# Attention with grouped heads on one core: a new instruction order, and the last head's norm and store in two halves

## The chip, the core and the metric

The kernel runs on one core of a Trainium2 chip. The core has a matrix engine (PE, TensorE), a vector engine (DVE, VectorE), an activation engine (ACT, ScalarE), a general engine (POOL, GpSimd) and a queue engine (SP, SyncE) that mostly issues DMAs. Each engine works through its own instructions in order and waits on semaphores for the others.

The metric is device time in microseconds (us), the median of several executions. Times inside an execution come from one profiled execution; its span runs from its first to its last instruction.

## What is computed

Softmax attention over 8 batches, 8 query heads and 2 key/value heads, a sequence of 1024 and a head size of 64, in float32 at the interface. Four query heads share one key/value head.

```python
scores = scale * np.matmul(q_group, k_group.transpose(0, 1, 3, 2))
scores_max = np.max(scores, axis=-1, keepdims=True)
attn = np.exp(scores - scores_max)
attn = attn / (np.sum(attn, axis=-1, keepdims=True) + 1e-08)
output[:, q_start:q_end, :, :] = np.matmul(attn, v_group)
```

The kernel leaves the maximum out, works in bfloat16 on the way, and gets the row sums from a column of ones beside V.

## The kernel before

**Heads and pairs.** There are 64 heads (batch times query head), numbered 0 to 63. A head's scores are made key-side first, in 8 pairs of 128 x 512 matmuls: one pair gives a 128 x 1024 tile `sp` in PSUM, and there are three such score buffers. So there are 512 score pairs. Each goes to one of two engines for its exponential:

- ACT: one exp activation (L764) into `pt`.
- DVE: a bit trick. One pass over the scores (L775, "dpass") writes 16-bit whole numbers `yt`. Two passes of up to 1024 scores form a *chain*, which is then finished in 16-bit steps: `zh` (L782, mantissa into `zt`), `two` (L789, exponent into `et`), `mul` (L798, `zt = yt * zt`) and, for the last `TAIL` heads alone, `add` (L803, `zt = et + zt`). The other heads have no add: PE multiplies both `et` and `zt` with V and so adds them in PSUM.

**Part of `mul` on GpSimd.** GpSimd can take columns of a chain's `mul` off DVE (L732, "gmul"). Its parts are placed beside a DVE pass, and beside a norm that follows it, and their widths are worked out by `gpsimd()` of the planner:

```python
until = t + window + M_GOVER
at += M_GLEAD
...
w = int((until - at - M_GFIX) / M_GCOL) // GSTEP * GSTEP
```

Here `window` is 1134 for a pass, plus `M_NORM` (531) where a norm follows, plus `M_REC` where it begins at a reciprocal. A part waits for the DVE instruction placed ahead of it.

**PV.** The probabilities are the stationary side of 128 x 65 matmuls with V (L816), for 8 pieces of 128 queries a head. Pieces are gathered by seven in one PSUM bank (`ops`), by four for the first head. A finished group gets a reciprocal of its sums (L881, "rec") and a multiplication (L890, "norm") into the ring `ost`, from which SP stores whole heads (L894). The first head (L836) and the last one (L856) are worked by key chunk rather than by piece. The last head's eight pieces lie in a freed score buffer, get one reciprocal and one norm of 128 x 512, and one store of 256 KB on SP's queue.

**The order.** A planner (`Plan`) replays the kernel with constants for the engines' costs (`M_ACT`, `M_REC`, `M_FIX`, ...), and reads from the text `ORDER` what PE and DVE do next. Letters of PE: `A` a score pair for ACT; `a` to `d` a score pair for DVE, of the current head or one to three heads on; `V` a group of PV matmuls; `E` and `L` the PV of the first and last head; `F` a filler matmul; `W` a planned wait. Letters of DVE: `p` and `P` a pass (`P` where a norm follows); `r` and `R` a reciprocal; `n` a norm; `0` to `3` the next step of that open chain; `i` idling. `x` closes an open chain. `W` and `i` issue nothing. What comes out is a list of events in planned time; the program is emitted in that order, so each engine's sequence is fixed, while the semaphores set the real times. DMA loads (GpSimd's cast copies `q`, `k`, `v`, SP's transposes and copies) and stores are placed by planned times as well.

Of the kernel before, what the change touches and what calls it, by code (L numbers as in the profile page):

```python
# [29 lines left out]
M_D1 = 1.042  # L30
M_D2 = 0.521
M_D4 = 0.261
M_REC = 90
M_GLEAD = 160
M_GFIX = 190
M_GCOL = 1.88
M_GOVER = 100
M_GLATE = 900
M_GFREE = 125
M_ISSUE = 850  # L40
M_OVER = 5000
NEED = 5150
M_GFREE = 125
M_OVER = 5000
NEED = 5150
M_NORM = 531
# [3 lines left out]
PB = 7  # L50
NPIECE = 8
GRAIN = 3
TAIL = 4
CHN = 2
LONG = 6
GFROM = 2
# [5 lines left out]


ORDER = """
AaApFFFFFWFFAWWWWWWWWWWWWWWWWWWWWaWWWWWWWWWWApEEWWAW0WWWbWWWWApEEWWAWW0WWWaEpAEWWA0WWAFWWWWbFF0FE0AE
pAWWWWWWWAR0AWWWWWWWWWaWWWnWWWWWWpWWWWAVVVVVVARnb0VVVVpAVVVVVA0aWWWWApVVVVVVVVAR0AVb0VVVPVVAVVVVnVVA
b0VVVpAVVVVVA0AWWW0WbVVVRVpVVVVAVVVnVVA0bWWWApVVVVVVVVA0AWW0WbVVVRVPVVVVAVVVnVVA0bWWWApVVVVVVVVA0cWW
0WAVVVRVPVVVVAVVVnVAb0WWWWWApVVVVVVVVA0AWW0WWcVVVRpVVVVVAVVnVVVA0bWWWApVVVVVVVVA1cWWWArVPVVVVVVVAnWc
WWA0VpVVVVVVVA0WWcWWApVVVVVVVVAR0AWWWc0VVVVVPVAVVVVVcnAVpVVVAVVV1WVVAcR0WWWWAVPVVVVVVVAnWWAWc0V1VVVV
VpVVAVVVA0bVRVPVVAVVVVVnAA0WVVVV1VVVVVV0AV0VVVVAbVRVPVAVVVVVVVnVAb0WWAVpVVVVVVVVVA0WWWbWA0VVVVVRVPVV  # L70
VAVVVVbnAVpVVVAVVVVV0VVAc1VVVApVVVVVVVA1WbWWWApVVVVVVVVVVA0r1bWWAPVVVVVVVVVAncW0WWAVVVV0VVARVPVVVVVV
AWWnWWWWbA1VVVVVpVVAVVVA1bVRVPVVVAVVVVnVAA00VVVVVAW0WbVVVpVVVVVVAVVrV0cAVpVVVVVAVV0VVAb0VVVVAPVVVVVV
VAncWWW0WAVVVVpVVVVAVVV0VAb0VVVRVpAVVVVVAnbWWW0WAVVVpVVVVAVVVRV1Ab1VVVVAPVVVVVVAnWbWWA0ipVVVVVVVVAR1
cVV1VAVPVVVVAVVVnVVA0bWWWApVVVVVVVVAR1cWWWAPVVVVVVVVVAnbWW0WAVVpVVVVVVVAVV0VVAAR1VVVVVnVVVVVV1cAVpVV
VVVVVA0WWWbWAVpVVVVVVVARWW1WbWWAVPVVVVVVVAnWWcWWA0VVV0VVVVVApVVVVVARW1WbWWAVPVVVVVVVAnWWcWWA0VVVpVVV
VVAVVRV1bAVPVVAVVVVnVAA0VVVV0VVVV0cWAVpVVVVVVVVARW1WbWWAVPVVVVVVVVVAnWcWWA0VVVVpVVVVVVAVV0VcARVPVVVA
VVVnVVA1bVVVpVAVVVVVA01cWWWApVVVVVVVVA0cVARPVVVVVVAnWAV0VVVVV1cWApVVVVVVVVA0cWWWA1VVVVRVPVVVAVVVVnVA
c0WWWApVVVVVVVVAR1cWWWAPVVVVVVVVAnAV1VVVVVVVc2AVpVVVVVVVVVArW0Wc1WWAVVVPVVVVVVAVVnVVVA2cVVpAVVVVVAR0
bVVPVAVVVVVVnAV2AAV1VVVV0VVVVVVA1bVRVPVVVVVAVVnVVVA0cVVVpAVVVVVAR1bWWWAPVVVVVVVVAncWWWA1VVVpVVVAVVVV
0VA1cVRVPVVAVVVVVVnVAa1WWWAVpVVVVVVVVVA0WWWcA1VVVVVpVVVVAVVVVV0VVAbWWWARpVVVVVVVAnAV1VVVVVV0VVVVA0cV  # L80
VVRVPAVVVVVVAnaWW0WWAVVVpVVVVVVAVV0VVA0bVVVVRPVVAVVVVAnWAV0VVVVVVV0bWAVpVVVVVVVARW0WbWAVPVVVVVVVAnWW
bWA0VVVVVpVVVVAVVVV0VVARb0WWWAVPVVVVVVVVVAnWWAWb0VVVVVpVVVAVVVVV0VVARb0WWWWAVPVVVVVVVAnWWbWWA0VVVVpV
VVAVVVV0VVA0bWWWARVPVVVVVVVAnWWbWWA0VVVVpVVVVAVVV0VVA0bWWWARVpVVVVVVVAnWbWWA0VVVVpVVAVVVVV0VVARb0WWW
AVPVVVVVVVAnWWaWWA0VVVVVpVVVVAVVVV0Aa0VVVVVpAVVVVVVAR0WbVVAPVVVVVVVAnAV1VVVVVV0VVAR0aVVVPVVAVVVAnbVi
VipVVVAVVVV0Ab0VVVVVApVVVVVVA0WbWWApVVVVVVVVVVAR1bWWWAPVVVVVVVVVAncWW0WAVpVVVVVVVA0WAVVRV1VVVVVVnVAb
1VVVVpAVVVVVA0bWWWARPVVVVVVVVAnbWWW1WAVVV1VVVVApVVVVVVA0WWbWWARpVVVVVVVVAnaWW1WAVVVpVVVVVAVV0VA0bVVV
RAPVVVVVVAnaV1AVVpVVVVAVVV0VVVAR0bWWWAPVVVVVVVVAnAV1VVVVVVV1VaAipVVVVVVVVVVA0WbWWARPVVVVVVVVVVAnAV1V
VVVVV1bWApVVVVVVVVVARW0WbWWWAPVVVVVVVVAnWbVV1VAVpVVVVVVAV0VVVVA0bWWRWAPVVVVVVVVAnAV1VVVVV1VVbAipVVVV
VVAWWRWW0WcAPVVVVVVVVAnWAWWWb1VVVVpVVVVAVVV0VVAR0cWWWAPVVVVVVVVAnWAWWWb1VVVV1VVVVApVVVVVAW0WWWcWARpV
VVVVVVVAnWcWWWA1VVVVpVVVVAVVV0VVA0cWWWARPVVVVVVVVAnbWWWA1VVVV1VVVVApVVVVVARWW0WbWAPVVVVVVVVAncWWWA1V  # L90
VVpVVVVVAVV0VVVAR0bWWWAPVVVVVVVVAnAV1VVVVVc1WAVpVVVVVVVA0WWbWARPVVVVVVVVAnWAV1VVVVVVb0WAVVpVVVVVVVVA
WW0WWWWcAVRPVVVVVVVAVnVVVb1AVVVpVVAVVVVA1cV0VVpAVVVVVVA1aWWWWARPVVVVVVVVAnbWWW1WAVVVpVVVVAVVVrV2AAnV
VVVV0VV1VVVVA0bVVVVVApVVVVVVVARWnWbWAVpVVVVVVVVVA0WAWWWA0VVVVVV0VVVVVVVrVnVbA0VVVVVVVVVApVVVVVAVV0VV
VAaVVVpVVAVVVVVV0AbWWWArPVVVVVVVVA0AVVnVVVVV0VVVVAAV0VVVVVVVVVVVARnaVVVpVAVVVVVVVVRA0AVnVVVVVV0VVVVV
VA0AVVVVVVVRVV0VVVVVVVVAanWWAVpVxVVVVVVVVVVAR0AWnWAVVV0VVVV0VVVVVL0LLLRnLLLLFFRFn
"""


# [339 lines left out]
def kernel(  # L438
# [7 lines left out]
    nc = tc.nc  # L446
# [239 lines left out]
    for x in [e for e in plan.ev if e[1] == "norm"]:  # L686
        lo, hi = x[2]
        for j in range(NJ - 1):
            if lo < (j + 1) * NPIECE <= hi:
                ev.append((x[0] + 700, "store", None, j, None))  # L690
        if lo >= plan.last:
            ev.append((x[0] + 1, "store", None, NJ - 1, None))
    order = {id(e): i for i, e in enumerate(ev)}
    ev.sort(key=lambda e: (e[0], order[id(e)]))

# [27 lines left out]
    for when, kind, x, j, c, *cols in ev:  # L723
# [101 lines left out]
        elif kind == "pvf":  # L825
            first = j == NC - 1
            if first:
                new_bank(0)
                new_bank(1)
            for i in range(NPIECE):  # L830
                par = i % 2
                ci = x if par == 0 else (x + NH) % NC
                every = [p for _, p in terms(0, par, [ci])]
                lo = i % 4 * (D + 1)
                for n, p in enumerate(every):
                    nc.tensor.matmul(  # L836
                        ops[i // 4][:, lo : lo + D + 1],
                        lhsT=p[:, i // 2 * 128 : (i // 2 + 1) * 128],
                        rhs=va[0][:, ci % NH, ci // NH, :],
                        start=(first and i % 4 == 0 and n == 0),  # L840
                        stop=(j == 0 and n == len(every) - 1),
                        skip_group_check=True,
                    )
        elif kind == "pvl":
            b, h = divmod(NJ - 1, H)
            first = j == NC - 1
            if first:
                new_slot(plan.spare)
            for i in range(NPIECE):
                par = i % 2  # L850
                every = [
                    (ci, p) for ci, p in terms(NJ - 1, par) if ci == (x if par == 0 else (x + NH) % NC)
                ]
                lo = i % 4 * (D + 1)
                for n, (ci, p) in enumerate(every):
                    nc.tensor.matmul(  # L856
                        sps[plan.spare][:, i // 4, lo : lo + D + 1],
                        lhsT=p[:, i // 2 * 128 : (i // 2 + 1) * 128],
                        rhs=va[(b * G + h // HPG) % NVA][:, ci % NH, ci // NH, :],
                        start=(first and i % 4 == 0 and n == 0),  # L860
                        stop=(j == 0 and n == len(every) - 1),
                        skip_group_check=True,
                    )
        elif kind in ("rec", "norm"):
            lo, hi = x
            n = hi - lo
            r = place_of(lo)
            if lo < plan.last:
                o = ops[plan.group_of[lo] % 2][:, 0 : n * (D + 1)]
                o = o.rearrange("p (s d) -> p s d", d=D + 1)  # L870
                sums = o[:, :, D]
            else:
                o2 = sps[plan.spare][:, :, 0 : 4 * (D + 1)]
                o2 = o2.rearrange("p b (s d) -> p b s d", d=D + 1)
                sums = o2[:, :, :, D]
            if kind == "rec":
                rec = rp.tile([128, NPIECE], FP32, name="rec")
                to = rec[:, 0:n]
                if lo >= plan.last:
                    to = to.rearrange("p (b s) -> p b s", b=2)  # L880
                vec = nc.vector.reciprocal(out=to, in_=sums)  # L881
            else:
                to, by = ost[:, r : r + n, :], rec[:, 0:n].unsqueeze(2).to_broadcast([128, n, D])
                if lo < plan.last:
                    o = o[:, :, 0:D]
                else:
                    o = o2[:, :, :, 0:D]
                    to = to.rearrange("p (b s) d -> p b s d", b=2)
                    by = by.rearrange("p (b s) d -> p b s d", b=2)
                vec = nc.vector.tensor_tensor(out=to, in0=o, in1=by, op=ALU.mult)  # L890
        elif kind == "store":
            b, h = divmod(j, H)
            r = place_of(j * NPIECE)
            ins = nc.sync.dma_start(  # L894
                out=rows(out[b, h], j in (0, NJ - 1)),
                in_=ost[:, r : r + NPIECE, :].rearrange("p (s two) d -> p s (two d)", two=2),
            )
            stores.append((when, ins))
# [30 lines left out]
```

## Time and profile before

| | us |
|---|---|
| median of 3 runs | 354.96 (354.9 to 355.17) |
| the profiled execution | 354.69 |
| its span | 352.9 |
| first exp on ACT starts | 6.22 |
| last matmul of the last head ends (L856) | 348.86 |
| last norm ends (L890) | 349.83 |

The time around the span (354.69 against 352.9) lies outside the instructions. The clock granted to PE was 1.000 over the whole execution. Share of the engines in the chain that ended last: DVE 67%, PE 21%, ACT 8%.

The forms of GpSimd's parts, which the sum of the change draws on (line, engine, operation, tiles, shapes and count | busy us, mean ns of one | idle before, releasers):

```profile
L732 POOL TENSOR_TENSOR zt<-yt,zt 128x464 bf16<-128x464 bf16 x66 | 70.1, 1063 | 53.7 <-DVE et L789 25.6 <-DVE zt L782 12.4 <-DVE zt L798 8.9
L732 POOL TENSOR_TENSOR zt<-yt,zt 128x800 bf16<-128x800 bf16 x28 | 47.5, 1698 | 25.4 <-DVE rec L881 14.9 <-DVE zt L782 3.9 <-DVE et L789 3.8
L732 POOL TENSOR_TENSOR zt<-yt,zt 128x752 bf16<-128x752 bf16 x28 | 45.0, 1608 | 24.9 <-DVE zt L782 15.9 <-PE sp L754 4.8 <-DVE et L789 3.4
```

How to read it: an engine's instruction may be issued before the record of the one ahead of it has ended, so records of one engine overlap a little, and the time an instruction costs is the distance from its start to the next start.

### The profile page before, as it was taken

What the parts mean: (1) busy time and instruction counts of PE and PEld (TensorE: products, weight loads), DVE (VectorE), ACT (ScalarE), POOL (GpSimd) and SP (SyncE); (2) the same over time, 40 slices, a digit from 0 to 9 for tenths busy, and PEclk for the clock granted to TensorE, in tenths of its full rate; (3) what the DMA queues carried; (4) which work ended last, traced back from release to release, by engine and by line L of the source; (5) the groups of instructions that cost most, each with busy time, mean ns of one, the idle gap of its engine ahead of it and who ended that gap; (6) DMA issues with size and microseconds to landing.
All of it is one profiled execution on the core that took longest, in us unless ns stands there. A gap on an engine that the chain in (4) does not pass through costs nothing.

```text
span 352.9 us, 14128 instructions
## 1 busy us (share of the span) xinstructions
PE 344.6 (98%) x6247; PEld 223.8 (63%) x6247; DVE 344.3 (98%) x519; ACT 344.3 (98%) x373; POOL 204.1 (58%) x188
## 2 busy tenths in 40 slices
PE   8899999999999999999999999999999999999995
PEld 4456666666666666666666666666666666666664
DVE  4999999999999999999999999999999999999995
ACT  5999999999999999999999999999999999999994
POOL 3157656676577666676766566666657676663000
PEclk9999999999999999999999999999999999999999
DMA  6799666478866987669639756679567885454133
GB/s 150 133 151 151 135 124 136 91 141 146 133 126 124 140 157 132 120 115 154 154 61 181 138 124 115 135 108 180 109 114 130 165 141 112 101 101 114 27 93 121
DMA packets 96430, 44.84 MB, mean 127 GB/s; under 512 B 61152, under 2 KB 95072, under 8 KB 95584
## 3 DMA queue, kind: packets, MB, share of 16 engines
q1 hardware_dynamic: 94128, 31.48, 43.1%
q0 software_dynamic: 2096, 12.19, 24.0%
q8 instruction: 49, 0.80, 1.1%
q10 hardware_dynamic: 144, 0.26, 0.2%
q14 instruction: 13, 0.11, 0.1%
HBM read 27.13 MB, written 28.97 MB: 159 GB/s over the span
## 4 chain that ended last, share of the span: by engine, by line
DVE 67%; PE 21%; ACT 8%; issue 3%; DVEq 0%
DVE yt L775 35%; PE ops L816 10%; DVE et L789 8%; PE sp L754 8%; ACT pt L764 8%; DVE zt L798 7%; DVE ost L890 7%; DVE zt L782 7%; DVE rec L881 2%; PE ops L619 1%; PE sp L856 1%; PE sp L642 0%; DVE kt L663 0%; PE ops L654 0%; PE ops L642 0%
## 5 line engine op out<-in xcount | busy, mean ns | idle before, releaser
L764 ACT ACTIVATE pt<-sp 128x1024 bf16<-128x1024 f32 x369 | 341.8, 1034 | 0.5 <-PE sp L754 0.4
L732 POOL TENSOR_TENSOR zt<-yt,zt 128x464 bf16<-128x464 bf16 (+5 forms) x131 | 173.4, 1324 | 107.7 <-DVE et L789 35.5
L816 PE MATMUL ops<-va,pt 128*128 128x65 bf16 x2848 | 175.1, 194 | 0.0
L754 PE MATMUL sp<-qt,kt 64*128 64x512 bf16 x1024 | 171.0, 382 | 3.2 <-ACT pt L764 1.5
L775 DVE TENSOR_SCALAR yt<-sp 128x1024 uint16<-128x1024 f32 x143 | 172.6, 1207 | 0.6 <-PE sp L754 0.5
L816 PEld LDWEIGHTS <-pt 128*128 128x128 bf16 x2848 | 127.7, 97 | 31.9 <-issue 31.9
L816 PE MATMUL ops<-va,zt 128*128 128x65 bf16 x1120 | 130.9, 194 | 0.0
L816 PE MATMUL ops<-va,et 128*128 128x65 bf16 x1072 | 121.7, 194 | 0.0
L816 PEld LDWEIGHTS <-zt 128*128 128x128 bf16 x1120 | 89.9, 97 | 12.3 <-issue 12.1
L816 PEld LDWEIGHTS <-et 128*128 128x128 bf16 x1072 | 84.2, 98 | 20.6 <-issue 20.6
L754 PEld LDWEIGHTS <-kt 64*128 64x128 bf16 x1024 | 49.2, 93 | 54.8 <-issue 32.5
L782 DVE TENSOR_SCALAR zt<-yt 128x2048 uint16<-128x2048 uint16 x72 | 50.1, 696 | 0.1
L789 DVE TENSOR_SCALAR et<-yt 128x2048 uint16<-128x2048 uint16 x72 | 49.6, 691 | 0.0
L798 DVE TENSOR_TENSOR zt<-yt,zt 128x832 bf16<-128x832 bf16 (+7 forms) x69 | 45.1, 654 | 0.0
L890 DVE TENSOR_TENSOR ost<-ops,rec 128x448 f32<-128x448 f32 (+2 forms) x73 | 44.3, 607 | 0.2
L517 POOL DMA_DIRECT2D qd<-in_q_dram x33 | 20.2, 613 | 4.2 <-PE sp L754 3.3
L881 DVE RECIPROCAL rec<-ops 128x7 f32<-128x7 f32 (+2 forms) x73 | 14.2, 195 | 0.0
L517 POOL DMA_DIRECT2D kd<-in_k_dram x8 | 5.4, 670 | 5.4 <-PE sp L754 5.4
L619 PE MATMUL ops<-warm 128*128 128x128 bf16 (+1 forms) x23 | 4.5, 339 | 1.2 <-DVE warm L511 1.2
L517 POOL DMA_DIRECT2D vd<-in_v_dram x8 | 5.0, 621 | 0.2 <-issue 0.2
L803 DVE TENSOR_TENSOR zt<-et,zt 128x2048 bf16<-128x2048 bf16 (+1 forms) x4 | 4.4, 1090 | 0.1
L619 PEld LDWEIGHTS <-warm 128*128 128x128 bf16 x23 | 2.0, 114 | 3.7 <-issue 2.5
(38 smaller groups left out, 25.2 us busy)
## 6 DMA issues: line engine op xcount, KB each, us to landing
out_dram<-ost SPq DMA_DIRECT2D x64, 256.0 KB, 3.1
qd<-in_q_dram POOLq DMA_DIRECT2D x29, 256.0 KB, 5.0
kt<-kt SPq DMA_DIRECT2D x30, 64.0 KB, 3.1
va<-vd SPq DMA_DIRECT2D x30, 64.0 KB, 3.7
kd<-in_k_dram POOLq DMA_DIRECT2D x7, 256.0 KB, 5.6
vd<-in_v_dram POOLq DMA_DIRECT2D x7, 256.0 KB, 5.2
qt<-qd SPq DMA_TRANSPOSE x63, 4.5
qd<-in_q_dram POOLq DMA_DIRECT2D x5, 128.0 KB, 3.7
```

What stands on the lines that cost most here:

```text
L517: return nc.gpsimd.dma_start(out=t.rearrange("(a x) d -> a (x d)", a=128), in_=src.rearrange("(a x) d -> a (x d)", a=128),)
L619: nc.tensor.matmul(ops[bank][:, lo : lo + cols], lhsT=warm[:, 0:128], rhs=warm[:, 0:cols], start=not beside, stop=True, skip_group_check=b ...
L732: gps = nc.gpsimd.tensor_tensor(out=z, in0=flat(yt[j])[:, lo : lo + w], in1=z, op=ALU.mult)
L754: now = nc.tensor.matmul(sps[x][:, half, :], lhsT=t[lo : lo + D, c // NH, ci % NH * 128 : (ci % NH + 1) * 128], rhs=qt[j][lo : lo + D, 0, ...
L764: exps.append(nc.scalar.activation(out=p, in_=where_s[(j, c)], func=AF.Exp, scale=scale))
L775: vec = nc.vector.tensor_scalar(out=yt[ch][:, i, :, :], in0=where_s[c], scalar1=EXP_A, scalar2=EXP_B, op0=ALU.mult, op1=ALU.add,)
L782: vec = nc.vector.tensor_scalar(out=zt[j][:, 0:c], in0=yt[j][:, 0:c], scalar1=0x7F, scalar2=0x3F00, op0=ALU.bitwise_and, op1=ALU.bitwise_or,)
L789: vec = ins = nc.vector.tensor_scalar(out=et[j][:, 0:c], in0=yt[j][:, 0:c], scalar1=0x7F80, scalar2=None, op0=ALU.bitwise_and,)
L798: vec = nc.vector.tensor_tensor(out=z, in0=flat(yt[j])[:, 0 : cols[0]], in1=z, op=ALU.mult)
L816: nc.tensor.matmul(ops[plan.group_of[x] % 2][:, lo : lo + D + 1], lhsT=p[:, qs * 128 : (qs + 1) * 128], rhs=va[(b * G + h // HPG) % NVA][: ...
L881: vec = nc.vector.reciprocal(out=to, in_=sums)
L890: vec = nc.vector.tensor_tensor(out=to, in0=o, in1=by, op=ALU.mult)
```

## The change

Three constants of the planner get other values: `M_REC` 90 to 115, `M_GOVER` 100 to 60, `M_GFREE` 125 to 85 (this one is the time by which a part may reach into the next DVE operation before the plan counts it as a delay). `TAIL` goes from 4 to 3, so head 60 loses its `add` step, and its `et` goes to PE. The text `ORDER` is a new one throughout. The last head's norm becomes two instructions of 128 x 256, one for each PSUM bank, and each is followed at once by its own store of 128 KB, the first on SP's queue, the second on ACT's; the store event of the last head is gone.

```diff
-M_REC = 90
+M_REC = 115
...
-M_GOVER = 100
+M_GOVER = 60
 M_GLATE = 900
-M_GFREE = 125
+M_GFREE = 85
...
-TAIL = 4
+TAIL = 3
...
 ORDER = """
-AaApFFFFFWFFAWWWWWWWWWWWWWWWWWWWWaWWWWWWWWWWApEEWWAW0WWWbWWWWApEEWWAWW0WWWaEpAEWWA0WWAFWWWWbFF0FE0AE
...
-VAaVVVpVVAVVVVVV0AbWWWArPVVVVVVVVA0AVVnVVVVV0VVVVAAV0VVVVVVVVVVVARnaVVVpVAVVVVVVVVRA0AVVnVVVVVV0VVVVV
-VA0AVVVVVVVRVV0VVVVVVVVAanWWAVpVxVVVVVVVVVVAR0AWnWAVVV0VVVV0VVVVVL0LLLRnLLLLFFRFn
+AaApFFFFWWWWFAWWWWWWWWWWWWWWWWWWWWWWWWWWWWaWWWWWWWWWWApEEWWAW0WWWbWWWWApEEWWAW0WWWaWWWWApEEWWA0WWbFF
...
+VVVVV0b0VVApVVVVVVVVAR0bWWWWAPVVVVVVVVVAnbW0WWAVVpVVVVVVAV0VVAARnVVVVV0VVVVVVVVA1AVVV1VVVVVV0VAAVVV
+RVV0VVVVVVVVAnAVVV0VVVVVVVVVVVVVVRAnaWWWApVVVVVVVVVxVA0ArVnVVVVVVV0VA0AVVV0VVVVVLLRnLLLLLWWLFFRFn
 """
...
-        if lo >= plan.last:
-            ev.append((x[0] + 1, "store", None, NJ - 1, None))
...
-                to, by = ost[:, r : r + n, :], rec[:, 0:n].unsqueeze(2).to_broadcast([128, n, D])
                 if lo < plan.last:
-                    o = o[:, :, 0:D]
+                    parts = [(nc.sync, 0, n, o[:, :, 0:D])]
                 else:
-                    o = o2[:, :, :, 0:D]
...
-                vec = nc.vector.tensor_tensor(out=to, in0=o, in1=by, op=ALU.mult)
+                    n //= 2
+                    parts = [(e, i * n, n, o2[:, i, :, 0:D]) for i, e in enumerate((nc.sync, nc.scalar))]
+                for e, i, m, src in parts:
+                    by = rec[:, i : i + m].unsqueeze(2).to_broadcast([128, m, D])
+                    to = ost[:, r + i : r + i + m, :]
+                    vec = nc.vector.tensor_tensor(out=to, in0=src, in1=by, op=ALU.mult)
+                    if lo >= plan.last:
+                        e.dma_start(
+                            out=rows(out[B - 1, H - 1], True)[:, i // 2 : (i + m) // 2, :],
+                            in_=to.rearrange("p (s two) d -> p s (two d)", two=2),
+                        )
```

Counts of letters in the two texts, which say how often each thing is done:

| | before | after |
|---|---|---|
| `A` (scores for ACT) | 369 | 370 |
| `a` to `d` (scores for DVE) | 143 | 142 |
| `0` to `3` (chain steps) | 220 | 219 |
| `p`, `P` (passes) | 89, 54 | 83, 59 |
| `r`, `R` (reciprocals) | 7, 67 | 4, 70 |
| `V` (PV groups) | 1616 | 1608 |
| `W` (planned waits of PE) | 406 | 436 |
| `F` (fillers) | 14 | 13 |

More of the change, by code (lines that the diff above doesn't have):

```diff
@@ L42 @@
 NEED = 5150
-M_GFREE = 125
+M_GFREE = 85
 M_OVER = 5000
@@ L64 @@
 ORDER = """
-AaApFFFFFWFFAWWWWWWWWWWWWWWWWWWWWaWWWWWWWWWWApEEWWAW0WWWbWWWWApEEWWAWW0WWWaEpAEWWA0WWAFWWWWbFF0FE0AE
[L66 to L94, printed above, removed]
@@ L95 @@
-VA0AVVVVVVVRVV0VVVVVVVVAanWWAVpVxVVVVVVVVVVAR0AWnWAVVV0VVVV0VVVVVL0LLLRnLLLLFFRFn
+AaApFFFFWWWWFAWWWWWWWWWWWWWWWWWWWWWWWWWWWWaWWWWWWWWWWApEEWWAW0WWWbWWWWApEEWWAW0WWWaWWWWApEEWWA0WWbFF
+WAFFpFEAWWW0WWWAAE0W0WWWWWWWWWWWWWWWaRAnWWWWRWWWPWAVVVVVVVVnA0bWWWWApVVVVVVVVA0aWVpAVVVVVAR0bVVA0VVV
+pVVVAVVVVnVAb0VVVApVVVAV0VVVVA0bVVRVPVAVVVVVAnbV0AVpVVVVVAVV0VVA0bVVRVPVAVVVVVAnbW0WWAVVpVVVVVVAV0VV
+VVA0bWWRWAPVVVVVVVVAnbW0WWAVVpVVVVAVVV0VVVVA0cWWWRWAPVVVVVVVVAnbW0WWAVVVpVVVAVVV0VVVVAR0cWWWAPVVVVVV
+VVAnbWW0WWAVVVpVVVVVAVV0VAc0VVVRVPAVVVVAnVA0WbVVVpVVVVAVVV0WVVA0bWWWWARPVVVVVVVVAncWWWA0VVVpVVVAVVVV
@@ new lines @@
+0VVA0bVVArPVVVVVVA0WcWWWAPVVVVVVVVAnAV0VVVV0VVVARb0VVVVPVVVAVVVVcnAVpVVVVVAVV0VVAb0VVVVRVAPVVVVVVAnW
+cWWWA0VVVVpVVVVAVVV1VVAc0VARVPVVVVVVAWnWWWbA0VVVVVpVAVVVVVV0VAc0WWWAVpVVVVVVVA0WbWWARVPVVVVVVVAnWWcW
+WA1VVVV0VVApVVVVVVVARWnWbWWApVVVVVVVVA0WcWWWApVVVVVVVVVA1cWWWARPVVVVVVVVVVAncWW1WAVVV2VVVVApVVVVVVVV
+VA00WcWWAVVRVPVVVVVAVVnVVVA1bWWWWApVVVVVVVVA0cWWRWAPVVVVVVVVAncWW01WWAVVpVVVVVVAWV0VcA1VVVVpVAVVVVAR
+0AVVc1VVVPVVVAVVVVnVAc1WWWWAVpVVVVVVVARWW0WcWWAPVVVVVVVVVAnWAV1VVVVVVVV1VcARVPVVVVVVAVnVVVA0cV1VVVVA
@@ new lines @@
+pVVVVVAW1WWWcWApVVVVVVVVA0cWWWARVPVVVVVVVAnWWcWWA1VVVVpVVVVAVVVVR0VAc1WWWAVPVVVVVVVAnWWcWA0VVVVVpVVV
+AVVVVRV0Ac1WWWAVPVVVVVVVAWnWWWcA0VVVVVpVVVAVVVV2AAV0VVVVVV0VbWWARPVVVVVVVVVVAncWWWA1VVVVpVVVVVAVVVVr
+V2VAc2WWWAVPVVVVVVVAnWWWbWA0VpVVVVVVVARWW2WcWWAVPVVVVVVVAnWWbWWA0VVVVpVVVVAVVV0VVAAWWRWWc0VVVVPVVVVA
+VVVnVAA1VVVVV1VVVVVA0bVVVVRVPVVVVAVVVVAnc1VVVApVVVVVVVVA1WWbWWApVVVVVVVVVVAR0c1WWWAVVPVVVVVVAVVnVVVV
+VA0bVVVpAVVVVVAR1bWWWWAPVVVVVVVVAncWW0WWAVVpVVVVVVAVV0VA1bVRVPVVAVVVVVnAA0VVVVV1VVVVVA0bVVpVAVVVVVVR
@@ new lines @@
+A1AVnVVVV1VbWWAipVVVVVVVVA0cWWWARPVVVVVVVVVAnbWWWA1VVVVpVVVVVAVVVV0cA0VVVVApVVVVVVVAR1AVVVnVVVVb1WWA
+VpVVVVVVVVA0WcWAVpVVVVVVVVAR0AWWWbVV0VVVVAPVVVVVVVAncWWARPVVVVVVVAnWWAV1VVVVVV0cWAVpVVVVVVVA1WAWWcRV
+nVVVVVpVVAVVVA01cVVpVAVVVVVV0AAWWW0WcVVVRVPVVVVAVVVnVVA1cWWWApVVVVVVVVA1AWWWbR0VVVVPVVVVAVVVnVVA1cWW
+WApVVVVVVVVAR0WcWWWAPVVVVVVVVAnAV1VVVVVb0WAVpVVVVVVVARW0WcWWAPVVVVVVVVAnbWWWA1VVV0VVVVVApVVVVVVA0WcW
+ARVPVVVVVVVVAnWAV1VVVVVVb0WWAVpVVVVVVVVVARW0WbWWAPVVVVVVVVVVAnAV1VVVVVVb0WAVpVVVVVVVVVARW0WAWWb0VVVV
@@ new lines @@
+VVPVVAVVVVVVVnVAb1WWAVpVVVVVVVA0WWbWARVPVVVVVVVAnWWAV1VVVVVV0VVVA1bVVVpVVAVVVVA0WbVRVPVVVAVVVVVAnA1W
+VVVVVV1VVcAipVVVVVVVVA0WWbVRAPVVVVVAnVVA1bVV1VVVVApVVVVVVA0WbWWARPVVVVVVVVAnAV1VVVVVb1WAVpVVVVVVVARW
+0WaWWAPVVVVVVVVAnbWWWW1WAVVVpVVVVVAVV0VVVA0aWWARPVVVVVVVVVAnAV1VVVVVVVb1AVpVVVVVVVVVARWW0WbWAPVVVVVV
+VAVnVVVVVV1VAb1WWWWAVpVVVVVVVVVA0WWbWARVPVVVVVVVVAnWWbWWA1VVVVVpVVVVAVVV1bAVpVVVVAVV0VAr1cVVPVVAVVVV
+AnAV1VVVVV0VVbARVpVVVVVVAWnWWWcWA1VVVVVpVVVAVVV0VVA0bWWWApVVVVVVVVAR1AWWWc1VVVVVPVVVAVVVVnVAb0WWWAVp
@@ new lines @@
+VVVVVVVARW1WAWWcV1VVVVVPVVAVVVVVnAc0WWWAVpVVVVVVVARWW1WbWAVPVVVVVVVAnWWcWA0VVVVpVVVAVVVV0cAVRpVVAVVV
+VVnVAb1WWWWApVVVVVVVVA0cWWWRWAPVVVVVVVVAnbWW1WWAVVVpVVVVVAVV0VVVARc0WWWAPVVVVVVVVAnbWW1WAVVVpVVVVVVA
+VV0VVAA0VVVV1VVVVVVVRc0AVPVVVVVVVAVnVVVA0bVVVApVVVVVVVVAR1AVVVnVVVVVV0VVVVA1aVVVpVAVVVVVVA0bWWWWARPV
+VVVVVVVAnbWWW1WAVVV1VVVApVVVVVVVA0WbWWARPVVVVVVVVAnbWWW1WAVVVpVVVVVAVV1VAA0VVV0VVVVVVVVVVARnbVVVVpVA
+VVVVVA0b0VVApVVVVVVVVAR0bWWWWAPVVVVVVVVVAnbW0WWAVVpVVVVVVAV0VVAARnVVVVV0VVVVVVVVA1AVVV1VVVVVV0VAAVVV
@@ L882 @@
             else:
-                to, by = ost[:, r : r + n, :], rec[:, 0:n].unsqueeze(2).to_broadcast([128, n, D])
                 if lo < plan.last:
-                    o = o[:, :, 0:D]
+                    parts = [(nc.sync, 0, n, o[:, :, 0:D])]
                 else:
-                    o = o2[:, :, :, 0:D]
-                    to = to.rearrange("p (b s) d -> p b s d", b=2)
-                    by = by.rearrange("p (b s) d -> p b s d", b=2)
-                vec = nc.vector.tensor_tensor(out=to, in0=o, in1=by, op=ALU.mult)
+                    n //= 2
[9 more added lines that the diff above has]
+                        )
         elif kind == "store":
@@ L894 @@
             ins = nc.sync.dma_start(
-                out=rows(out[b, h], j in (0, NJ - 1)),
+                out=rows(out[b, h], j == 0),
                 in_=ost[:, r : r + NPIECE, :].rearrange("p (s two) d -> p s (two d)", two=2),
```

## The prediction

> **What bounds the kernel now.** I read the page's busy shares first, then its groups, the waits, the timeline, and last the end of the span.
>
> ```profile
> PE 344.6 (98%) x6247; PEld 223.8 (63%) x6247; DVE 344.3 (98%) x519; ACT 344.3 (98%) x373; POOL 204.1 (58%) x188
> ...
> L764 ACT ACTIVATE pt<-sp 128x1024 bf16<-128x1024 f32 x369 | 341.8, 1034 | 0.5 <-PE sp L754 0.4
> L775 DVE TENSOR_SCALAR yt<-sp 128x1024 uint16<-128x1024 f32 x143 | 172.6, 1207 | 0.6 <-PE sp L754 0.5
> L881 DVE RECIPROCAL rec<-ops 128x7 f32<-128x7 f32 (+2 forms) x73 | 14.2, 195 | 0.0
> ```
>
> Three engines show 98%. The exps on ACT and the passes on DVE share out the 512 score pairs (369 and 143), and both engines sit idle for about half a us in all. But a busy share hides short pauses, because records overlap: an instruction is issued before the last one's record has ended. So the number to use is start to start. In the timeline of ACT, early and late:
>
> ```profile
> 6.22 8.36 ACT L764 ACTIVATE pt<-sp 128x1024 bf16<-128x1024 f32 x9 [0.40 <-PE sp L754]
> ...
> 259.66 20.70 ACT L764 ACTIVATE pt<-sp 128x1024 bf16<-128x1024 f32 x22
> ```
>
> The first run has a record of 1.03 on its end: (8.36 - 1.03)/8 = 0.916 us from exp to exp. The second has (20.70 - 1.03)/21 = 0.937. Over all 369, busy is 341.8, so 0.926. ACT therefore loses 341.8 - 369 x 0.916 = 3.8 us in pauses too short to count as idle. DVE has none of its own:
>
> ```profile
> 80.72 0.68 DVE L789 TENSOR_SCALAR et<-yt 128x2048 uint16<-128x2048 uint16 x1
> 81.32 0.19 DVE L881 RECIPROCAL rec<-ops 128x7 f32<-128x7 f32 x1
> 81.43 1.17 DVE L775 TENSOR_SCALAR yt<-sp 128x1024 uint16<-128x1024 f32 x1
> 82.52 0.61 DVE L890 TENSOR_TENSOR ost<-ops,rec 128x448 f32<-128x448 f32 x1
> 83.05 0.77 DVE L782 TENSOR_SCALAR zt<-yt 128x2048 uint16<-128x2048 uint16 x1
> 83.74 1.21 DVE L775 TENSOR_SCALAR yt<-sp 128x1024 uint16<-128x1024 f32 x1
> ```
>
> Every start follows the one before by that operation's own cost: 0.60, 0.11 (the reciprocal: the plan of before says M_REC = 90 ns), 1.09, 0.53, 0.69. The 0.69 for zt is a stretched one: the same form takes 0.60 elsewhere. POOL tells why:
>
> ```profile
> 81.58 1.69 POOL L732 TENSOR_TENSOR zt<-yt,zt 128x800 bf16<-128x800 bf16 x1 [0.99 <-DVE rec L881]
> ```
>
> This part ends at 83.27, inside the zt operation that began at 83.05. So DVE is the engine that runs late against the order it was planned in. PE, which issues everything in one fixed order, passes the lateness on: it waits for a score buffer from DVE, then comes late to ACT's next score. That chain is my reading. The chain of waits supports it with DVE 67% and ACT 8%.
>
> The end of the span, from the timeline:
>
> ```profile
> 348.90 0.21 DVE L881 RECIPROCAL rec<-sp 128x8 f32<-128x8 f32 x1 [0.42 <-PE sp L856]
> 349.14 0.69 DVE L890 TENSOR_TENSOR ost<-sp,rec 128x512 f32<-128x512 f32 x1
> 349.86 0.34 SPq L894 DMA_DIRECT2D out_dram<-ost  x1
> ```
>
> The last exp ends at 348.12 (ACT's last run of 11 starts at 337.64 and takes 10.48), the last norm at 349.83, the span at 352.9. By the times of its DMA packets, the store's 256 KB move from 350.70 to 351.48.
>
> **What the Trainium skill says.** "SBUF — State Buffer", section "Who interferes with whom": VectorE in a two-port mode, or with two SBUF inputs, and GpSimd exclude each other for a whole instruction; one PSUM input keeps VectorE off the shared pair. The trace agrees: parts run beside passes and norms (PSUM inputs), and the zt above is stretched by 0.09. "VectorE: DVE Perf Modes", section "The perf-mode tier table": 693 ns for a bf16 tensor_scalar of 2048 and 1224 for a tensor_tensor; the trace has 0.69 and 1.22 as records, some 0.08 less from start to start. "DMA: Bandwidth & Descriptors", section "Issuing engines are not separate DMA queues": another issuing engine saves the issue time alone. Here the transfer of 0.78 us is the part to split; no run shows it yet.
>
> **The change part by part.** Operations are counted from the letters of ORDER.
>
> 1. Passes and exps. A goes from 369 to 370, a to d together from 143 to 142. ACT: +0.92. DVE: one pass less, -1.13 (its mean start to start).
> 2. Chains. TAIL = 3 gives head 60 the short form. With two passes each in heads 60 to 62 and one in 63, before has 7 pairs with an add (L803: three of 2048, one of 1024); now 5 (two and one): -1.14. Heads 0 to 60 have 137 pairs, odd, so one more chain holds a single pair: zt and et each lose a half (0.69 to 0.43 as records), -0.52.
> 3. GpSimd. The window formula in gpsimd() gives the widths of before exactly: 464, 752 (norm follows), 800 (from the reciprocal). With M_GOVER 60 and M_REC 115 it gives 448, 728 and 792. The text has 33 passes behind an R (30 before), 27 lone P (29), 81 lone p (82, of which 73 had a part). So about 33 x 792 + 27 x 728 + 65 x 448 + 7 x 410 = 77,800 columns, against 78,912 summed over before's forms. DVE multiplies 142 x 1024 - 77,800 = 67,600 columns, against 67,520: +0.05, give or take 0.5, because the leftovers of a chain can't be read from the text. That is: shorter parts, but more of the long kinds.
> 4. Port stretch. Set beside unstretched ones of their kind, record by record, the fast operations behind the 131 parts take 2.5 us more in sum: about 52 ns behind an 800, 31 behind a 752, 2 behind a 464. Parts 15 to 45 ns shorter (1.88 ns a column) leave about 37, 5 and 0: 33 x 37 + 27 x 5 = 1.4. So -1.1; bounds -2.5 and 0.
> 5. Reciprocals and norms: 74 each in both. The constant M_REC itself changes no instruction; it makes the plan fit 0.115, where 74 x 25 ns = 1.85 us of lateness had piled up unplanned.
> 6. Last norm in halves: two records of 256 elements (0.42 each as in row L890's 128x256) with 0.35 between, 0.77 for 0.69: +0.08. The first half's store starts 0.35 earlier and moves 128 KB in 0.39, all but done when the second needs the DMA engines. After the second norm half only 0.39 of data instead of 0.78: -0.39. The ACT queue has nothing left to do, so nothing stands behind its wait. Smaller pieces per partition could cost 0 to 0.2, one more queue to wait for at the end about 0.06 (the step between SP's last waits). Net about -0.25.
> 7. PE: head 60 has two more short-form pairs, one pair less elsewhere: +8 PV matmuls at 0.03 = 0.25, on an engine whose row of waits shows 32.5 us before score weights. I take nothing; 0.25 if that cover is gone.
> 8. DMA loads keep their number and rules; they move with the new order, and SP's and POOL's queues with them. Waits for loads in before are only at the start. Taken at nothing; up to 1 us if a transpose comes late once.
>
> DVE sum: -1.13 - 1.14 - 0.52 + 0.05 - 1.1 + 0.08 for the halves = -3.8. With before's 0.6 idle kept, its last norm could end at 349.83 - 3.8, about 346.1.
>
> ACT sum: first exp at 6.22 as before (the code ahead of it is the same), 370 x 0.916 + 0.11 of the last record: 345.25 without pauses; call the pauses g. Behind the last exp: 0.46 for PE's 8 matmuls, 0.28 for the reciprocal, 0.77 for the halves, so 1.51 (before: 1.71, since PE was still busy). Then 0.86 to the first packet, 0.39 of data, 1.42 to the span's end, 0.06 for the extra wait. Span = 345.25 + g + 4.24 = 349.5 + g. With before's g of 3.8 that is 353.3, 0.4 longer than now. All the gain lies in g, and ACT, not DVE, is late next.
>
> How much of g goes? DVE's lateness goes, but its floor (346.1) is only 0.7 below ACT's (346.8), so two streams of nearly one length stay coupled through PE and three score buffers. I take a third of g as staying, 1.3: span 350.8, that is -2.1. Against the profiled 354.69 this makes 352.6; the median of the runs is 0.27 above that execution, so 352.8.
>
> **Rivals.**
> - Pauses all but vanish (g = 0.3): 351.8. For it: DVE's work falls by more than the 3.8 lost. Against: the floors are close. 0.12.
> - PE is the cause of most pauses: a score that waits behind a group of PV matmuls stays late whatever DVE does, g = 2.5: 354.0. For it: the chain's last 45 us go mostly through PE. Against: PE waits on buffers that DVE frees. 0.20.
> - Slower: one exp more on a stream whose pauses don't shrink. ACT pays 0.92, the tail gives 0.54 back, and the shift of scores in a different order makes g 4.3: 355.8. It is slower by over 0.2% from g = 4.1 on. For it: ACT is at 98% with no idle to take the exp in. Against: it needs DVE's relief to reach ACT nowhere. 0.08.
> - The change doesn't do what it says: the stretch stays at 2.5. DVE's floor is then 347.2, above ACT's; g would be nearer 2: 353.5. It lies within the first and third cases.
>
> **How the numbers follow.** The likeliest, 0.60: 352.8, own range 352.1 to 353.6. About 0.2% or 0.7 us is what a measurement can tell from no change, so faster means under 354.25. Faster: 0.60 + 0.12 + 0.12 of the PE case = 0.84; same: the rest of it and a little of the slower one, 0.09; slower 0.07. The range leaves out the slower case, the upper edge of the PE case and the lowest of the first: 351.5 to 354.5.
>
> **What would show it.** Right: ACT x370 with a busy time near 340.2 and 0.919 from start to start; DVE L775 x142, L803 x3; zt and et medians near 0.68 with maxima under 0.75; DVE idle of 1 to 3 us waiting for scores; the last two norm records 0.35 apart, the last data packet 1.3 after the second. Wrong: ACT's pitch still 0.926 or above with DVE idle (PE is the cause), or DVE still without idle (my sum is off).

## The result and the profile after

The changed kernel takes 353.62 us (353.44 to 354.78), the kernel before 354.91: a ratio of 0.997, 95% interval 0.996 to 0.998. Measured a second time beside other kernels it took 353.05 against 354.67: 0.9957, interval 0.9945 to 0.997. A third measurement, of after_ahead, which turned out to be the same sequence of instructions, gave 353.37: 0.9966, interval 0.9954 to 0.9978. So it is faster by 1.3 to 1.6 us; 2.1 had been predicted. The three ratios differ by 0.0013, some 0.5 us, so a smaller difference between two kernels can't be told from noise.

The page of the changed kernel, the rows that answer to those of before (engine busy shares; then line, engine, operation, tiles, count | busy us, mean ns | idle before):

```profile
PE 344.3 (98%) x6254; PEld 223.7 (64%) x6254; DVE 342.6 (97%) x518; ACT 343.5 (98%) x374; POOL 199.8 (57%) x189
...
L762 ACT ACTIVATE pt<-sp 128x1024 bf16<-128x1024 f32 x370 | 341.0, 1038 | 0.7 <-PE sp L752 0.5
...
L773 DVE TENSOR_SCALAR yt<-sp 128x1024 uint16<-128x1024 f32 x142 | 171.4, 1207 | 0.7 <-PE sp L752 0.5
L780 DVE TENSOR_SCALAR zt<-yt 128x2048 uint16<-128x2048 uint16 (+1 forms) x72 | 50.2, 697 | 0.2
L787 DVE TENSOR_SCALAR et<-yt 128x2048 uint16<-128x2048 uint16 (+1 forms) x72 | 48.7, 681 | 0.0
L796 DVE TENSOR_TENSOR zt<-yt,zt 128x872 bf16<-128x872 bf16 (+12 forms) x69 | 45.4, 660 | 0.0
...
L801 DVE TENSOR_TENSOR zt<-et,zt 128x2048 bf16<-128x2048 bf16 (+1 forms) x3 | 3.1, 1041 | 0.0
```

ACT does one exp more than before in 0.8 us less. At 0.916 us an exp, 370 of them need 338.9; the busy time of 341.0 leaves pauses of 2.1, where before had 3.8. That is the gain. The chain that ended last shows what took DVE's place (67% DVE before):

```profile
PE 45%; ACT 34%; DVE 18%; issue 1%; DVEq 0%
```

The span's end, from the timeline of DVE and of ACT:

```profile
346.44 0.56 DVE L889 TENSOR_TENSOR ost<-ops,rec 128x384 f32<-128x384 f32 x1
348.02 0.21 DVE L879 RECIPROCAL rec<-sp 128x8 f32<-128x8 f32 x1 [1.02 <-PE sp L854]
348.26 0.76 DVE L889 TENSOR_TENSOR ost<-sp,rec 128x256 f32<-128x256 f32 x2
```

```profile
346.42 1.07 ACT L762 ACTIVATE pt<-sp 128x1024 bf16<-128x1024 f32 x1
349.05 0.35 ACTq L891 DMA_DIRECT2D out_dram<-ost  x1
```

DVE now waits 1.02 us for PE ahead of the last reciprocal (0.42 before), the two norm halves take 0.76 together, and ACT's queue issues the second store at 349.05. From the last exp's end (347.49) to the span's end it is 4.34 us, against 4.80 before.

A balance of the two profiled executions, each term from the trace:

| term | predicted | measured |
|---|---|---|
| start of the first exp | 0 | +0.17 |
| one exp more | +0.92 | +0.92 |
| ACT's pauses | -2.5 | -1.74 (3.77 to 2.03) |
| last exp to span's end | -0.54 | -0.46 |
| span | -2.1 | -1.1 |

### The profile page after: what moved, and what is told of

The parts are those of the page before. It is cut to its first block, busy times and chain, and to the rows that moved or that the text cites. A ratio compares the mean times of both kernels' runs of the same rounds, so it can differ in the third digit from the quotient of the medians.

```text
span 351.8 us, 14155 instructions
## 1 busy us (share of the span) xinstructions
PE 344.3 (98%) x6254; PEld 223.7 (64%) x6254; DVE 342.6 (97%) x518; ACT 343.5 (98%) x374; POOL 199.8 (57%) x189
## 4 chain that ended last, share of the span: by engine, by line
PE 45%; ACT 34%; DVE 18%; issue 1%; DVEq 0%
ACT pt L762 34%; PE ops L814 24%; PE sp L752 19%; DVE yt L773 10%; DVE zt L780 2%; DVE ost L889 2%; DVE et L787 2%; DVE zt L796 2%; PE ops L619 1%; PE sp L854 1%; DVE rec L879 1%; PE sp L642 0%; PE ops L654 0%; DVEq L928 0%; PE ops L642 0%
## 5 line engine op out<-in xcount | busy, mean ns | idle before, releaser
L762 ACT ACTIVATE pt<-sp 128x1024 bf16<-128x1024 f32 x370 | 341.0, 1038 | 0.7 <-PE sp L752 0.5
L730 POOL TENSOR_TENSOR zt<-yt,zt 128x448 bf16<-128x448 bf16 (+6 forms) x132 | 168.4, 1276 | 110.2 <-DVE et L787 41.2
L814 PE MATMUL ops<-va,zt 128*128 128x65 bf16 x1112 | 128.8, 194 | 0.0
L814 PEld LDWEIGHTS <-zt 128*128 128x128 bf16 x1112 | 88.2, 97 | 11.6 <-issue 11.6
L780 DVE TENSOR_SCALAR zt<-yt 128x2048 uint16<-128x2048 uint16 (+1 forms) x72 | 50.2, 697 | 0.2
L787 DVE TENSOR_SCALAR et<-yt 128x2048 uint16<-128x2048 uint16 (+1 forms) x72 | 48.7, 681 | 0.0
L796 DVE TENSOR_TENSOR zt<-yt,zt 128x872 bf16<-128x872 bf16 (+12 forms) x69 | 45.4, 660 | 0.0
L517 POOL DMA_DIRECT2D qd<-in_q_dram x33 | 21.3, 646 | 5.0 <-PE sp L752 4.2
L801 DVE TENSOR_TENSOR zt<-et,zt 128x2048 bf16<-128x2048 bf16 (+1 forms) x3 | 3.1, 1041 | 0.0
```

The source lines that it names most:

```text
L517: return nc.gpsimd.dma_start(out=t.rearrange("(a x) d -> a (x d)", a=128), in_=src.rearrange("(a x) d -> a (x d)", a=128),)
L730: gps = nc.gpsimd.tensor_tensor(out=z, in0=flat(yt[j])[:, lo : lo + w], in1=z, op=ALU.mult)
L762: exps.append(nc.scalar.activation(out=p, in_=where_s[(j, c)], func=AF.Exp, scale=scale))
L780: vec = nc.vector.tensor_scalar(out=zt[j][:, 0:c], in0=yt[j][:, 0:c], scalar1=0x7F, scalar2=0x3F00, op0=ALU.bitwise_and, op1=ALU.bitwise_or,)
L787: vec = ins = nc.vector.tensor_scalar(out=et[j][:, 0:c], in0=yt[j][:, 0:c], scalar1=0x7F80, scalar2=None, op0=ALU.bitwise_and,)
L796: vec = nc.vector.tensor_tensor(out=z, in0=flat(yt[j])[:, 0 : cols[0]], in1=z, op=ALU.mult)
```

## The experiments

Two questions: what the halves of the last norm bring, and what the pauses of ACT are made of, before and after. In the theory called D in the expectations, DVE is late and PE passes that on; in P, PE is late by its own PV groups.

The code ahead of the first exp is the same in every kernel, yet its start lay between 5.76 and 6.60 us in the profiles. A single span carries that accident, so the table takes it off. Pauses are summed from the exps' starts in the trace, over 0.916 us each. Ratios are to the kernel before, measured beside it.

The pauses mix two things that the traces can tell apart. Call the time from one exp's start to the next a step. A step is *late* where the last signal that the exp waits for, nearly always PE's that the scores are done, came within 40 ns before its start, so that ACT had nothing to start on sooner; otherwise the scores were *ready*. The shortest steps that occur often take 0.904 us. The 0.916 of the prediction is a mean that contains some late ones, so pauses of nothing don't mean that no exp waits. "Late" is the sum over 0.904 us of the late steps, "ready step" the mean length of the others.

| kernel | median us | ratio, 95% interval | ACT's pauses | late | ready step | span less first exp |
|---|---|---|---|---|---|---|
| before | 354.91 |  | 3.8 | 6.0 | 0.914 | 346.7 |
| before_halves | 354.70 | 1.0001 (0.9992 to 1.001) | 3.8 | 5.8 | 0.914 | 346.9 |
| before_mul48 | 353.54 | 0.9969 (0.9958 to 0.998) | 2.5 | 4.8 | 0.914 | 345.4 |
| before_lightpe | 353.84 | 0.9978 (0.9971 to 0.9986) | 2.9 | 6.2 | 0.908 | 346.0 |
| before_cut_lightpe | 351.98 | 0.9923 (0.9909 to 0.9936) | 0.8 | 3.9 | 0.909 | 343.9 |
| changed | 353.62 | 0.997 (0.996 to 0.998) | 2.0 | 4.3 | 0.913 | 345.4 |
| after_again | 353.05 | 0.9957 (0.9945 to 0.997) | 2.0 | 4.2 | 0.913 | 345.3 |
| after_whole | 353.68 | 0.9968 (0.9956 to 0.9981) | 2.0 | 4.2 | 0.914 | 345.7 |
| after_mul48 | 353.00 | 0.9959 (0.9946 to 0.9971) | 1.6 | 3.6 | 0.914 | 345.3 |
| after_cut | 352.87 | 0.9945 (0.9932 to 0.9957) | 1.6 | 3.6 | 0.914 | 344.9 |
| after_lightpe | 352.38 | 0.9928 (0.9914 to 0.9942) | 1.2 | 4.1 | 0.909 | 344.5 |
| after_cut_lightpe | 351.62 | 0.9912 (0.9899 to 0.9926) | 0.3 | 3.6 | 0.908 | 343.6 |
| after_trim32 | 353.16 | 0.9956 (0.9943 to 0.9968) | 1.7 | 4.0 | 0.913 | 345.0 |
| after_ahead | 353.37 | 0.9966 (0.9954 to 0.9978) | 2.0 | 4.1 | 0.914 | 345.4 |

From the kernel before to the changed one, late falls from 6.0 to 4.3 us, as much as the pauses do, and the ready steps keep their length: the gain is exps that wait less for their scores.

**The halves alone, and the order alone.** The first adds the change's new norm and stores to the kernel before; the second puts the single norm and store back into the changed kernel:

```diff
-vec = nc.vector.tensor_tensor(out=to, in0=o, in1=by, op=ALU.mult)
+parts = [(e, i * n, n, o2[:, i, :, 0:D]) for i, e in enumerate((nc.sync, nc.scalar))]
...
```

> The kernel before with the last norm and store in halves alone; order and constants stay. My sum: the last 128 KB of data in place of 256 KB, less a second norm record, 0.25 to 0.4 us less than before (354.91), so about 354.6. Rival (the halves make the whole gain): 353.6. Rival (the store's end is fixed latency, halving brings nothing): 354.9.

> The changed kernel with one last norm and one store again. My sum: 0.25 to 0.4 us above the changed kernel (353.62), so 353.9 to 354.0: most of the gain is the order's. If the halves make the whole gain: 354.9. If they make nothing: 353.6.

> The changed kernel itself, beside the others of this call. Any theory: 0.997 of before, as it was measured first (353.62 against 354.91). It is the base for the three others, and settles whether the halves of the last norm bring anything over one norm (0.9968 of before).

In the old order the halves bring nothing. In the new one the time with them and without them can't be told apart (0.9957, 0.9966 and 0.997 against 0.9968), so the gain is that of the order with its constants and `TAIL`. The profiles show a part for the halves all the same. In the window of the last stores, first before_halves, then the changed kernel (queue that issued, KB each, us from issue to landing):

```profile
out_dram<-ost SPq DMA_DIRECT2D x1, 128.0 KB, 2.5
out_dram<-ost ACTq DMA_DIRECT2D x1, 128.0 KB, 2.0
```

```profile
out_dram<-ost SPq DMA_DIRECT2D x1, 128.0 KB, 1.8
out_dram<-ost ACTq DMA_DIRECT2D x1, 128.0 KB, 1.8
```

The first half, meant to be out of the way, took 2.5 us in the old order and landed last of all. The SP queue's timeline tells why, again before_halves and then the changed kernel:

```profile
345.91 2.73 SPq L898 DMA_DIRECT2D out_dram<-ost  x2
349.36 0.70 SPq L891 DMA_DIRECT2D out_dram<-ost  x1
```

```profile
344.66 2.73 SPq L898 DMA_DIRECT2D out_dram<-ost  x2
348.71 0.34 SPq L891 DMA_DIRECT2D out_dram<-ost  x1
```

The store of head 62, the second of the two in the line above, is issued about 1.1 us before the first half in the old order, and 1.7 us before in the new one; its 256 KB go in packets of 512 bytes. In before_halves the last of these ends at 350.74. The first half's own data, issued at 349.36, begin at 350.68, after 1.32 us; those of the second half, on ACT's queue, begin 0.86 us after their issue. In the changed kernel the first half's data begin 0.84 us after their issue, as those of the single store did before (349.86 to 350.70). From the last norm's end to the span's end: 3.09 before, 3.25 with halves in the old order, 3.11 with one norm in the new order, 2.82 with both.

The distance of the issues alone doesn't decide. In after_mul48, with halves and 1.7 us too, the first half's data begin after 1.13 us and the stretch takes 3.06. What goes with the gain is when head 62's last packet ends: 0.9 to 1.1 us behind the first half's issue in the changed kernel, after_again, after_cut, after_trim32 and after_ahead (2.75 to 2.82), 1.3 and 1.4 us in after_mul48 and before_halves (3.06 and 3.25). So the halves are worth some 0.3 us in a profile, but only where the store ahead of them is out in time.

**Less stretch.** The long GpSimd parts end sooner:

```diff
 lo, w = c
+if w >= 600:
+    w -= 64
```

> The changed kernel; every GpSimd part of 600 columns or more ends 64 columns (120 ns) sooner, and these columns are left out: their product is not formed, DVE gets no more work. Theory D (the parts reach into DVE's next operation, DVE runs late, PE passes that on to ACT): stretch from 1.8 us to about 0.3, pauses of ACT from 2.0 to about 1, time 352.3 to 352.9. Theory P (PE is late by its own PV groups): the stretch goes, the pauses stay at 2.0, time 353.6.

The stretch fell (2.0 to 0.8 us, summed from the records), the pauses to 1.6 rather than 1, and late from 4.3 to 3.6. The ratio, 0.9945, is below all three of the changed kernel, but by no more than these differ. Theory D has a part in the late steps; a gain in time isn't clear of the noise.

**Less PE work.** Most PV matmuls of `et` are left out (840 of 1,096 in the changed kernel, 832 of 1,088 in the kernel before):

```diff
 ci, p = every[i]
+if 0 < i < len(every) - 1 and every[i + 1][0] == ci and job > 0:
+    continue
```

> The changed kernel without most PV matmuls of et (all but the first of a piece; from head 1 on), about 27 us of PE's time; the result lacks those terms. Theory P: PE reaches every score in time, ACT's pauses fall from 2.0 to under 0.5, time about 352.0. Theory D: PE waits for DVE's buffers as before, pauses stay at 1.5 or more, time 353.1 to 353.6.

> The kernel before without most PV matmuls of et (all but the first of a piece; from head 1 on). The same cut took pauses from 2.0 to 1.2 in the changed kernel. If DVE's lateness holds PE through the score buffers here: pauses stay above 2.7, under 1 us below before. If PE's own groups are the cause: pauses under 1.5, over 2 us below before.

In the changed kernel the pauses fell to 1.2, between the two expectations; in the kernel before to 2.9 with a gain of 0.7 us, as expected if DVE holds PE. That looks like a share of PE in the changed kernel alone, but the pauses fell by the same 0.8 to 0.9 in both, and late in neither: 6.0 to 6.2 before, 4.3 to 4.1 after. What became shorter are the steps whose scores were ready, from 0.914 to 0.908 and from 0.913 to 0.909. So PE's own groups aren't shown to make scores late in either kernel. Why an exp that has its scores goes faster beside a PE with less to do, no run shows.

What PE does with its new time is seen in its row, of before_lightpe and then of after_lightpe:

```profile
L754 PE MATMUL sp<-qt,kt 64*128 64x512 bf16 x1024 | 177.3, 382 | 20.1 <-DVE yt L775 11.8
```

```profile
L752 PE MATMUL sp<-qt,kt 64*128 64x512 bf16 x1024 | 178.0, 382 | 17.4 <-DVE yt L773 7.7 <-ACT pt L762 4.1
```

It waits for score buffers, from DVE more than from ACT; in the kernel before and in the changed one this row shows 3.2 and 2.7 us in all, since the time goes to PV groups there.

**Both.**

> The changed kernel with both cuts at once: long GpSimd parts 64 columns shorter (left out), and most PV matmuls of et left out. The cuts alone took 0.75 us (DVE) and 1.24 us (PE) off and left pauses of 1.6 and 1.2 of 2.0 us. Theory of two causes (DVE's lateness and PE's own groups each give a share): pauses under 0.5, 1.6 to 2.0 us below the changed kernel. Theory of one chain (either cut frees the same pauses): no better than the PE cut alone, 1.2 to 1.3 us below.

> The kernel before with both cuts: long GpSimd parts 64 columns shorter (left out) and most PV matmuls of et left out. In the changed kernel both left pauses of 0.3. If that is all there is here too: pauses 0.3, span less first exp about 343.3, one exp less than there. If the reciprocals' lateness is a third cause: pauses 1.5 to 2, since these cuts do not touch it.

With both cuts the pauses of the changed kernel are 0.3, the number of the theory of two causes. The steps don't bear it out: late is 3.6, as with the shorter parts alone, and the ready step 0.908, as with the lighter PE alone. So the waits are not gone; the shorter steps beside them hide them in the sum. Here is a run of 29 exps that are still (26.81 - 1.03)/28 = 0.921 us apart:

```profile
249.09 26.81 ACT L764 ACTIVATE pt<-sp 128x1024 bf16<-128x1024 f32 x29
```

In the old order pauses of 0.8 are left, not the 1.5 to 2 that a third, separate cause would leave, and late is 3.9. There the cut of the parts on top of the lighter PE took 1.9 us (353.84 to 351.98) and 2.2 us of late; in the new order 0.6 us (0.9928 to 0.9912) and 0.6 us of late. A part of that difference is the dose, since the parts had more stretch to lose in the old order (2.7 us against 2.0).

**Less DVE work, the same dose in both.**

```diff
 elif kind == "mul":
+    cols = [cols[0] - 48]
```

> The kernel before; each of DVE's 69 multiplications leaves 48 columns out, so DVE has 69 x 25 ns = 1.7 us less to do, spread over the run: the size of the 74 x 25 ns by which the reciprocals outlast their constant. My step 5 (that unplanned lateness makes the pauses): pauses from 3.8 to about 2.0, 1.3 to 1.8 us below before. Rival (PE's own groups make the pauses): pauses stay above 3, less than 0.7 us below before.

> The changed kernel with the same 48 columns left out of each of DVE's 69 multiplications. If DVE's lateness is mostly planned for now: under 0.7 us below the changed kernel, pauses from 2.0 to 1.5. If DVE still sets the pace: 1.3 us or more below it.

This tells the two kernels apart best. 1.7 us less on DVE are worth 1.0 us in the kernel before (pauses 3.8 to 2.5, late 6.0 to 4.8), between what I expected and what the rival said. DVE also leaves the chain that ended last, where it had 67%:

```profile
ACT 62%; PE 35%; DMA 1%; DVE 1%; issue 0%
```

In the changed kernel the same dose is worth nothing that can be measured in time (0.9959, between 0.9957 and 0.997). Late falls there too, by 0.7 us, of which the slower end of the stores (3.06 instead of 2.82) takes back 0.2. Before, DVE set the pace; after, the same relief shortens ACT's waits by about half as much.

**Two tries at a faster kernel.** In the first, 32 columns of each long part that begins at a reciprocal go back to DVE; in the second, ACT's score pairs were to go ahead of the PV group in front of them where their buffer is planned free.

```diff
+cut = 32 if e[0] in recs and w >= 600 else 0
+ev[i] = (*e[:4], (lo + was + cut, w - cut))
...
+if s[0] - at > 100 + 20:
+    ev[i] = (s[0] - 100, *s[1:])
```

> The changed kernel; each long GpSimd part that begins at a reciprocal is 32 columns shorter, and DVE multiplies these columns: nothing is left out. 27 parts x 60 ns sooner takes about 1.5 us of stretch away and gives DVE 27 x 32 x 0.52 ns = 0.45 us of work. Theory D: DVE 1.0 us less late, 0.4 to 0.7 us below the changed kernel. Rival (the stretch lies on DVE's spare time): within 0.2 us of it.

> The changed kernel; a score pair for ACT goes ahead of the PV group before it on PE wherever its score buffer is planned free 120 ns or more before. No work changes. Theory P (a share of the pauses is PE inside a PV group when ACT's buffer is long free): pauses from 2.0 to about 1, 0.6 to 1.2 us below the changed kernel. Rival (the pauses come from waits for buffers): no change, or slower by PE waiting at the buffer instead of doing PV.

Neither is faster than the changed kernel beside it (353.16 and 353.37 against 353.05). The second one is the changed kernel: its edit makes 230 planned times of scores 100 ns earlier, but in the plan a score stands at least 160 ns behind the start of the PV group in front of it, so none went ahead, and PE's matmuls follow each other in the trace as in the changed kernel. It says nothing for or against theory P, which stays untested in this form.

The trim did what it should to the stretch. The changed kernel, with a part that runs from 120.21 to 121.90, and the trimmed one, whose part ends at 121.23:

```profile
121.70 0.75 DVE L780 TENSOR_SCALAR zt<-yt 128x2048 uint16<-128x2048 uint16 x1
122.37 1.21 DVE L773 TENSOR_SCALAR yt<-sp 128x1024 uint16<-128x1024 f32 x1
```

```profile
121.10 0.69 DVE L792 TENSOR_SCALAR zt<-yt 128x2048 uint16<-128x2048 uint16 x1
121.71 1.21 DVE L785 TENSOR_SCALAR yt<-sp 128x1024 uint16<-128x1024 f32 x1
```

The zt step costs 0.67 and 0.61 from start to start. Over the run the stretch fell from 2.0 to 0.8 us, but the columns given back cost DVE 0.5 us, so its relief was about 0.7 rather than 1.0. Late fell by 0.3, and the time lies between 353.05 and 353.37, two measurements of the changed kernel: too small a dose to show in it.

## Why the prediction was right, and where it was off

- **The mechanism held for the kernel before.** "All the gain lies in g": the extra exp cost its 0.92, the tail gave back 0.46 of the predicted 0.54, and the pauses paid for all of it. before_mul48 shows the link from DVE's load to ACT's waits, which had only been argued. There 1.7 us less on DVE took 1.3 us of late; the change also took 1.7 us off DVE (below), and 1.7 us of late. That suggests that DVE's relief makes most of the gain. Whether the rest comes from where the new order places PE's work is not shown.
- **The size of g was off: 2.0, not 1.3.** That is 0.7 of the 1.0 us between predicted and measured span (350.8 and 351.8); 0.17 is the start of the first exp and 0.08 the tail. That a third of g would stay was a judgement, with no sum behind it; more than half stayed. The median came out 0.8 above the forecast, just past the upper end of the likeliest case's own range.
- **The DVE sum was the weakest step: -3.8 predicted, -1.7 measured** (from start to start, without visible idle). Passes -0.9 instead of -1.13 and adds -1.15 instead of -1.14 were nearly right. The rest was not:
  - Step 3: DVE multiplies 69,184 columns, not 67,600. I took every reciprocal with a pass behind it as the start of a part, 33; 27 parts of 792 came of it, 25 of 728 and 69 of 448. That is 0.8 us.
  - Step 4: the stretch fell by about 0.7, not 1.1. Behind a 792 it is some 56 ns, not 37. Of the 800s, 10 of 28 began less than 180 ns after their reciprocal's start and reached about 125 ns into the next operation; of the 792s only 6 of 27 begin so soon, the others mostly about 250 ns after, so that the median reach fell only from 200 to 190 ns. One part alone reached 472 ns and cost 0.34 us.
  - Step 5: three more reciprocals are followed at once by their own norm, which waits for them: 0.23 us from start to start instead of 0.11, some 0.35 in all, and readable from DVE's letters (an `R` with `n` next), which I had not counted.
- **One of its own signs of being wrong came true.** DVE was to wait for scores 1 to 3 us; it waits 0.7, as before (0.6). With -1.7 in the sum, DVE's floor would have been 348.1, well above ACT's 346.8. For a floor above ACT's the prediction had g near 2 and 353.5, and that is what was measured. The likeliest case came near it with a gain on DVE twice too large, so it is in part luck that its range held.
- **"ACT, not DVE, is late next" was half right.** DVE's share of the last chain fell from 67% to 18%, and its relief is worth less. But it still shortens ACT's waits by 0.7 us (after_mul48), and a lighter PE doesn't shorten them. What makes the other late steps of the changed kernel, 3.6 us of 4.3, is open.
- **The PE rival, g = 2.5 and 354.0,** said that a score behind a group of PV matmuls stays late whatever DVE does. In the kernel before it is wrong as the main cause: late falls with less work on DVE, and not with less on PE. In the changed kernel no run bears it out either.
- **The rival that slower follows from one exp more** needed pauses that don't shrink; they did.
- **Halves: -0.25 predicted.** The working missed that head 62's store is on the same queue just ahead. In the new order it has room, and the tail came near the sum; the same edit in the old order is worth nothing. The statement cited there, that another issuing engine saves the issue time alone, isn't borne out here. In before_halves it saved more: the half on SP's queue waited 1.32 us for its first data, the one on ACT's 0.86.
- **Open:** whether the new value of the reciprocal's constant or simply a better search made the order fit. The order is read against the planner's times, letter by letter, so that text and constants can't be exchanged one by one; it was not tried.

## What to carry to other kernels

When three engines show 98%, ask which one's relief the others answer to: take the same small dose of work from one engine in both versions and compare. Then split the consumer's steps by whether its input came last: a sum of pauses can shrink because the other steps became shorter. And look in the trace whether an edit changed the order of instructions at all, before its unchanged time is read as an answer. Halving a last store helped here only where the store ahead of it on that queue was out in time.

## What was not expected

- The first exp started 5.76 to 6.60 us into the span in kernels with the same opening code, an accident as large as some of the effects looked for.
- A lighter PE made the exps whose scores were ready 4 to 5 ns shorter each, over 1 us in a run, and left the late ones as they were.
- A GpSimd part delays DVE's next operation only by what it reaches into it beyond some 130 ns. In the kernel before, a reach of 100 to 125 ns cost about 6 ns, of 175 to 200 ns 56, of 200 to 225 ns 82. Parts of 464 columns reached 86 ns at the median and cost next to nothing, so shortening them to 448 could bring nothing.
